# Scores of two heads: six 64-row matmuls replaced by four 128-row matmuls on stacked halves

## The chip, the cores and the metric

The kernel runs on one core of a Trainium2 chip. The metric is the device time of one execution in microseconds; the median of three runs before the change is 1390.06 us (1389.64 to 1392.08). The names of the engines in the rows: PE is TensorE, DVE is VectorE, ACT is ScalarE, POOL is GpSimd, and SP is the engine that issues the transfers.

## What is computed

A decoder trunk of two layers on a sequence of 1024 rows of width 1024, float32. Layer A is differential attention with 8 heads of two 64-wide components, layer B is stick-breaking attention with 16 heads of width 64; the kernel takes those in 8 pairs, so in either layer one unit of work ("a head" below) holds two 64-wide score products. Cut from the reference:

```python
# layer A, per block of 128 query rows: two softmaxes, one difference
def probs(qb, k):
    s = jnp.einsum('bhqd,bshd->bhqs', qb, k).astype(jnp.float32) * scale
    return jax.nn.softmax(jnp.where(mask, s, -jnp.inf), axis=-1)
a = probs(qb1, k1) - lam * probs(qb2, k2)
return jnp.einsum('bhqs,bshe->bhqe', a.astype(v.dtype), v)

# layer B, per block of 128 query rows
z = jnp.einsum('bhqd,bshd->bhqs', qb, k).astype(jnp.float32) * scale
log_beta = jax.nn.log_sigmoid(z)
log_1mb = jnp.where(mask, jax.nn.log_sigmoid(-z), 0.0)
suffix = lax.cumsum(log_1mb, axis=3, reverse=True) - log_1mb
a = jnp.where(mask, jnp.exp(log_beta + suffix), 0.0)
return jnp.einsum('bhqs,bshe->bhqe', a.astype(v.dtype), v)
```

Around them stand an input norm and projections to q, k, v and a gate, and an output projection that is added to the residual. Layer B's keys and values come from a projection of the residual after layer A.

## The kernel before

Every float32 product is made of three products of a narrower 4-byte type (F32R): each operand is split into a high part (ACT copies it into F32R) and a low part (DVE subtracts the copy from the original), and high by high, high by low and low by high are added in PSUM; low by low is left out. A projection group (`group`, L567) is 24 such matmuls of 512 columns or 24 of 256 columns into one of two PSUM banks ("proj").

Work goes head by head. While one head's attention runs, the projections of the next head are merged between its steps as filling for PE. A head's attention is four units m of two blocks of query rows each; `unit_s` makes scores and the row work of DVE and ACT, `unit_t` transposes the result and multiplies it with v. `VISITS` (L612) cuts the scores of a head into ten visits: five of one block with 512 key columns, three of one block with 384, and two of two blocks (256 and 256 columns, and again 256 and 256). A visit is one filling of the PSUM tile `sc` (two banks, one for each 64-wide component).

`scores` (L619) issues a visit as six matmuls per block. The two components c lie on partitions 0 to 63 and 64 to 127 (`HI`), so each matmul uses 64 rows of the array, and the two of one term stand side by side on the two halves of it: three terms by two components. A trace row such as `sc<-kh,q 64*128 64x512 x2` is one term of both components. After the visit `evac` empties the banks: in layer A with one DVE instruction per component, in layer B with ACT copies, one for both components where the block is at most 512 columns long, else one per component.

q and k come from `split_q` and `split_k` (L657, L660): one ACT copy and one DVE subtraction each on all 128 partitions for 512 columns, twice per head for q and twice for k. The sources are PSUM banks: `tr` (transposed rows) in layer A, `proj` in layer B.

The order on every engine is set before the run by a planner (`Order.issue`, L271): it gives each operation a duration (`cost`, L240), walks through time, and lets each engine take the ready operation of the lowest number; buffers of a pool are handed out in order and block what finds none free. For PE it adds 0.42 us to each group that begins with a 64-row matmul (L200). A `rec.together()` block is one operation for it and stays in one piece. Buffers that the change touches: `o` (attention output and gate, 6), `small` (8), `zl` in layer A (score rows, 6), `q` (4 per part), `sc` (one tile of two banks).

Of the kernel before, what the change touches and what calls it, by code (L numbers as in the profile page):

```python
# [25 lines left out]
HALF = 512  # L26
EPS = 1e-6
BIG = 1.0e30
# [4 lines left out]
def f32(ap):  # L33
    return ap.bitcast(F32)
# [345 lines left out]
def build(tc, ins, out):  # L380
    nc = tc.nc
    rec = Order(tc, {"pe": nc.tensor, "act": nc.scalar, "dve": nc.vector, "pool": nc.gpsimd, "sp": nc.sync})
    act, dve, pool, pe, sp = (rec.engine(e) for e in ("act", "dve", "pool", "pe", "sp"))
# [3 lines left out]
    w_vg, w_qk, w_kv, w_b = ins["w_vg"], ins["w_qk"], ins["w_kv"], ins["w_b"]  # L387

    mk = lambda name, bufs, **kw: ctx.enter_context(tc.tile_pool(name=name, bufs=bufs, **kw))
    B = {"proj": 2, "sc": 2, "tr": 3, "av": 1, "th": 3, "g2ka": 2, "g2kb": 3, "o": 6, "w": 8, "raw": 4, "ta": 1, "g1k": 2, "hpr": 1, "small": 8, "qk": 2, "hpe": -1, "hpw": -1,  # L390
         "al": 6, "bl": 8, "tb": 3, "oa": 0, "la": 0, "lb": 8, "lt": 0, "lead": 1.0, "leada": 0.02, "leadb": 0.02, "leadxa": 0.15, "leadxb": 0.1, "holda": 0, "holdb": 0, "c2": 1, "gca": 0, "gcb": 0, "prea": 2, "preb": 1, "warm": 16, "wp": 2, "hpx": -1, "nx": 1, "nk": 6, "hpo": 0, "ob": 2, "late": 400, "ahead": 0}
    ORDERS = ((0, 1, 2, 3), (3, 0, 2, 1), (1, 3, 0, 2), (2, 0, 3, 1), (3, 2, 1, 0), (1, 2, 0, 3), (0, 2, 1, 3), (2, 3, 0, 1),
              (1, 0, 3, 2), (3, 2, 0, 1), (2, 3, 1, 0), (1, 0, 2, 3))
    cp = mk("const", 1)
# [31 lines left out]
    def fixed(pool, shape, dt, name):  # L426
        return L(Root(shape, dt, "sbuf", pool, real=pools[pool].tile(shape, dt, name=name)))
# [1 line left out]
    def kept(shape, name):  # L429
        return L(Root(shape, F32, "dram", "dr", real=dr.tile(shape, F32, name=name)))  # L430

    zt = lambda: T("zl", [P, S], B["al"], pool=layer[0])

    def zbt():

        return T("zl", [P, S + 4], B["bl"], pool=layer[0])

    def zat(n):
        return zt()

    t1k = lambda: T("t1k", [P, 256], B["ta"], pool=layer[0])
    g1k = lambda: T("g1k", [P, 256], B["g1k"], pool=layer[0])
    u4k = lambda: T("u4k", [P, S], B["tb"], pool=layer[0])
    g2k = lambda: T("g2k", [P, HALF], B["g2k" + "ab"[layer[1]]], pool=layer[0])
    small = lambda n: T("small", [P, 16], B["small"])[:, :n]

    def C(name, shape, dt=F32):
        return fixed("cp", shape, dt, name)
# [8 lines left out]
    mask_a = fixed("la", [P, HALF], mybir.dt.bfloat16, "mask_a")  # L457
    pool.memset(mask_a, 0.0)
    pool.affine_select(mask_a[:, 384:], mask_a[:, 384:], [[-1, P]], ALU.is_ge, BIG, base=0, channel_multiplier=1)


    warm = PS("tr", B["tr"])
# [155 lines left out]

    def scores(hd, visit, evac):  # L619

        n_t[0] += 1
        pts = T("sc", [P, 2, 512], 1, pool="ps")
        col = 0
        with rec.together():
            for i, off, w in visit:
                rs_ = slice((i % 4) * P, (i % 4) * P + P)
                q, wm = hd.q[i // 4], max(w, 256)
                for a, b in ((0, 0), (0, 1), (1, 0)):
                    for c in range(2):
                        pe.matmul(pts[:, c, col:col + wm], q[a][HI[c], rs_], hd.k[b][HI[c], off:off + wm], start=(a + b == 0),  # L630
                                  stop=(a == 1))
                col += wm
        col = 0
        for i, off, w in visit:
            evac(i, off, w, pts[:, :, col:col + w])
            col += max(w, 256)

    def s_steps(hd, m, evac, chain):
# [7 lines left out]

        return [(sum(4 * w * 0.42 for _, _, w in visit), lambda v=visit, d=done: step(v, d)) for visit, done in VISITS[m]]

    def split_rows(h, l, pt, scale):

        act.activation(h, pt, AF.Copy, scale=1.0 if scale is None else scale)
        if scale is None:
            dve.tensor_tensor(l, pt, f32(h), ALU.subtract)
        else:
            dve.scalar_tensor_tensor(l, pt, scale, f32(h), ALU.mult, ALU.subtract)

    def split_k(k, sl, pt, scale):  # L657
        split_rows(k[0][:, sl], k[1][:, sl], pt, scale)

    def split_q(q, pt, scale):  # L660
        split_rows(q[0], q[1], pt, scale)

    def transposed(ae, ao, t, last):

# [86 lines left out]
            hd.k = (T("kh", [P, S], 2, F32R), T("kl", [P, S], 2, F32R))  # L751

    def alloc_q(hd, hf):
        hd.q[hf] = [T(f"q{i}", [P, HALF], 4, F32R) for i in range(2)]
        return hd.q[hf]

    def gate_steps(hd, xT, r):
# [16 lines left out]
    class OutProj:  # L774
# [43 lines left out]
        def load_rest(self):  # L818
            w = {}
            for kc in range(self.nk, KC):  # L820
                w[kc] = [T(t, [P, HALF], 4, F32R) for t in ("q0", "q1")]
                k = slice((kc - 6) * 256, (kc - 5) * 256)
                if layer[1]:
                    for i in range(2):
                        sp.dma_start(f32(w[kc][i]).rearrange("p (c n) -> p c n", c=2),
                                          self.w_out[0:2, i, :, kc * 256:(kc + 1) * 256].rearrange("c p n -> p c n"))
                    continue
                split_w([t.unsqueeze(1) for t in w[kc]], self.w_out[0:2, 3, :, k].rearrange("c p n -> p c n"))
            return w
# [193 lines left out]
    def unit_s_a(h, m):  # L1023
        hd = heads_a[h]

        def evac(qb, off, w, pts):
            n = (qb + 1) * P
            if qb not in hd.rows:
                hd.rows[qb] = [zat(n + P), zat(n + P)], [small(2), small(2)]
            p, mn = hd.rows[qb]  # L1030
            k = 0 if off == 0 else 1
            mask = mask_a[:, HALF - w:] if off + w == n else mask_a[:, 0:1].to_broadcast([P, w])
            for c in range(2):
                dve.tensor_tensor_reduce(p[c][:, off:off + w], pts[:, c, :], mask, 1.0, BIG, ALU.add, ALU.min,
                                         mn[c][:, k:k + 1])

        def chain(qb):
            n = (qb + 1) * P
            p, mn = hd.rows[qb]
            s = small(2)  # L1040
            for c in range(2):
                b = mn[c][:, 0:1]
                if n > 512:
                    dve.tensor_tensor(b, b, mn[c][:, 1:2], ALU.min)
                act.activation(p[c][:, :n], p[c][:, :n], AF.Exp, bias=b, scale=-1.0, accum_out=s[:, c:c + 1])
            r = small(2)
            dve.reciprocal(r, s)
            dve.tensor_tensor(r[:, 1:2], r[:, 1:2], nlam, ALU.mult)
            dve.tensor_scalar(p[0][:, :n], p[0][:, :n], r[:, 0:1], None, ALU.mult)
            dve.scalar_tensor_tensor(p[1][:, :n], p[1][:, :n], r[:, 1:2], p[0][:, :n], ALU.mult, ALU.add)  # L1050
            hd.at[qb] = p[1]

        return s_steps(hd, m, evac, chain)
# [68 lines left out]
        split_x(1, i)  # L1122
    squares(1)

    cst = zt()
    sp.dma_start(cst[:, :256], ins["rope"])
    sp.dma_start(cst[:, 256:544], ins["rows"].to_broadcast([P, 288]))
    rope = cst[:, :256].rearrange("p (r i d) -> p r i d", r=8, i=2)
# [104 lines left out]
    def unit_s_b(p, m):  # L1233
        hd = heads_b[p]

        def evac(qb, off, w, pts):
            n = (qb + 1) * P
            heads = ((0, 1),) if n <= HALF else ((0,), (1,))
            w2 = len(heads[0]) * n
            if qb not in hd.rows:  # L1240
                hd.rows[qb] = [zbt() for _ in heads]
                for t in hd.rows[qb]:
                    pool.memset(t[:, w2:w2 + 1], 0.0)
            for t, cs in zip(hd.rows[qb], heads):
                t3 = t[:, :w2].rearrange("p (c n) -> p c n", c=len(cs))
                with hp():
                    act.activation(t3[:, :, off:off + w], pts[:, cs[0]:cs[-1] + 1, :], AF.Copy)
                if off + w == n:
                    pool.affine_select(t3[:, :, n - P:], t3[:, :, n - P:], [[0, len(cs)], [-1, P]], ALU.is_ge, -BIG,
                                       base=-1, channel_multiplier=1)  # L1250

        def chain(qb):
            n = (qb + 1) * P
            z = hd.rows[qb]
            w2 = n * 2 // len(z)
            for t in z:
# [100 lines left out]
```

## Time and profile before

| | |
|---|---|
| median of three runs | 1390.06 us |
| the profiled execution | 1398.29 us |
| its span, first to last instruction | 1396.4 us |
| mean granted TensorE clock over it | 0.99 of full |
| busy: PE / DVE / ACT / POOL | 97% / 78% / 64% / 26% |
| chain of work that ended last, share on PE | 69% |

The profiled execution is 8.2 us longer than the median run. PE's busy share counts the pipelined tail of a matmul as busy, so how fast PE works is read from the distance between the starts of neighbouring matmuls, not from their durations. Nearly all rows carry the line L377, since one statement issues everything; tiles tell the groups apart.

### The profile page before, as it was taken

Reading aid. Unit: us, or ns where it says so; the run is one execution under the profiler, and the core shown is the slowest. Engines: PE = TensorE matmul, PEld = TensorE weight load, DVE = VectorE, ACT = ScalarE, POOL = GpSimd, SP = SyncE. Lnnn points to the kernel's source line nnn. Section 1 sums busy time; section 2 is a strip of 40 time slices with the busy share of each in tenths; the row PEclk is TensorE's granted clock in tenths of the full one; section 3 lists DMA queues with packets and bytes.
Section 4 is the critical chain, followed back from the end, with each engine's and each line's share of the span. In section 5 each row is a group of like instructions: output and inputs, shape, how many; then the busy total and the mean of one; then the engine's idle time right before and its main releaser. Section 6 shows DMA issues by size and latency. Waiting matters only on the chain.

```text
span 1396.4 us, 23006 instructions
## 1 busy us (share of the span) xinstructions
PE 1360.2 (97%) x8160; PEld 1126.5 (81%) x8160; DVE 1091.8 (78%) x2015; ACT 889.2 (64%) x1734; POOL 364.0 (26%) x589
## 2 busy tenths in 40 slices
PE   8999999999999999999899999999999999999988
PEld 7998979797979788768787878778787878788767
DVE  7689798888888987766744789797979696989771
ACT  7476657666767575533325687787778786877540
POOL 4412232322223223103201132332324142323100
PEclk8999999999999999999999999999999999999999
DMA  5255546554646465651523112121212121156624
GB/s 190 69 174 174 181 139 195 166 175 149 203 147 188 151 214 191 204 199 61 174 68 121 61 69 84 61 91 61 91 61 91 61 90 51 62 190 216 231 80 139
DMA packets 99395, 185.83 MB, mean 133 GB/s; under 512 B 8912, under 2 KB 43472, under 8 KB 98256
## 3 DMA queue, kind: packets, MB, share of 16 engines
q1 hardware_dynamic: 99280, 184.35, 40.3%
q8 instruction: 65, 1.06, 0.3%
q14 instruction: 50, 0.41, 0.1%
HBM read 119.31 MB, written 65.01 MB: 132 GB/s over the span
## 4 chain that ended last, share of the span: by engine, by line
PE 69%; DVE 15%; ACT 5%; DMA 4%; issue 4%; POOL 2%; SPq 0%; DVEq 0%; POOLq 0%; ACTq 0%
PE proj L377 46%; PE av L377 8%; PE tr L377 8%; PE sc L377 7%; DVE u4k L377 6%; DVE zl L377 3%; ACT zl L377 2%; DMA w_b<-raw 1%; DVE tl L377 1%; DVE o L377 1%; DVE small L377 1%; POOL qk L377 1%; ACT u4k L377 1%; DMA raw<-in_b_w_out_dram 1%; DMA raw<-in_w_b_dram 1%
## 5 line engine op out<-in xcount | busy, mean ns | idle before, releaser
L377 PE MATMUL proj<-ah,w 128*128 128x512 f32 x2016 | 701.3, 405 | 7.5 <-DVE w L377 2.2
L377 PEld LDWEIGHTS proj<-ah,w 128*128 128x128 f32 x2016 | 381.3, 189 | 99.4 <-issue 15.9
L377 PE MATMUL proj<-al,w 128*128 128x512 f32 x1008 | 396.5, 393 | 0.2 <-DVE al L377 0.2
L377 PEld LDWEIGHTS proj<-al,w 128*128 128x128 f32 x1008 | 191.6, 190 | 29.8 <-DVE al L377 0.5
L377 PE MATMUL proj<-w,ah 128*128 128x256 f32 x1024 | 198.4, 292 | 1.2 <-ACT ah L377 0.7
L377 DVE TENSOR_TENSOR_SCAN u4k<-zl,u4k 128x768 f32<-128x768 f32 (+4 forms) x96 | 181.5, 1891 | 3.1
L377 DVE TENSOR_TENSOR tl<-tr,th 128x512 fp32r<-128x512 f32 (+1 forms) x240 | 144.9, 629 | 42.7 <-ACT th L377 39.4
L377 PEld LDWEIGHTS proj<-w,ah 128*128 128x128 f32 x1024 | 162.0, 194 | 6.8 <-issue 4.1
L377 ACT ACTIVATE u4k<-u4k 128x768 f32<-128x768 f32 (+4 forms) x192 | 158.3, 841 | 7.3 <-DVE u4k L377 4.9
L377 ACT ACTIVATE th<-tr 128x512 fp32r<-128x512 f32 (+1 forms) x240 | 124.9, 549 | 50.6 <-PE tr L377 44.8
L377 PE MATMUL av<-th,v 128*128 128x256 f32 x640 | 152.4, 293 | 4.7 <-ACT th L377 2.8
L377 PE MATMUL proj<-w,al 128*128 128x256 f32 x512 | 147.1, 287 | 1.8 <-DVE al L377 1.5
L377 PE MATMUL sc<-kh,q 64*128 64x512 f32 (+2 forms) x768 | 140.2, 382 | 1.0 <-DVE small L377 1.0
L377 PE MATMUL av<-tl,v 128*128 128x256 f32 x480 | 130.7, 292 | 7.8 <-DVE tl L377 7.5
L377 PEld LDWEIGHTS av<-th,v 128*128 128x128 f32 x640 | 111.4, 191 | 24.2 <-issue 7.1
L377 PE MATMUL tr<-ident,zl 128*128 128x128 f32 x864 | 128.8, 274 | 1.3 <-DVE zl L377 0.8
L377 PEld LDWEIGHTS tr<-ident,zl 128*128 128x128 f32 x864 | 101.3, 141 | 14.7 <-issue 4.4
L377 DVE SCALAR_TENSOR_TENSOR u4k<-zl,u4k 128x768 f32<-128x768 f32 (+4 forms) x96 | 94.2, 981 | 23.6 <-ACT u4k L377 22.6
L377 POOL TENSOR_SCALAR_AFFINE_SELECT zl<-zl 128x128 f32<-128x128 f32 (+1 forms) x96 | 71.9, 766 | 154.6 <-ACT zl L377 136.3
L377 POOL TENSOR_TENSOR o<-o,o 128x512 f32<-128x512 f32 (+1 forms) x56 | 87.5, 1562 | 93.0 <-DVE o L377 93.0
L377 PEld LDWEIGHTS sc<-kh,q 64*128 64x128 f32 x768 | 69.8, 184 | 49.5 <-issue 25.1
L377 DVE CUSTOM_DVE_ANT_0 zl<-sc,mask_a 128x384 f32<-128x384 f32 (+3 forms) x192 | 99.4, 550 | 12.2 <-PE sc L377 12.0
(136 smaller groups left out, 2005.5 us busy)
## 6 DMA issues: line engine op xcount, KB each, us to landing
w_kv<-raw SPq DMA_DIRECT2D x64, 256.0 KB, 2.7
w_b<-raw SPq DMA_DIRECT2D x64, 256.0 KB, 3.0
w<-w_kv SPq DMA_DIRECT2D x32, 512.0 KB, 5.3
w<-w_b SPq DMA_DIRECT2D x32, 512.0 KB, 4.9
w<-w_o SPq DMA_DIRECT2D x24, 512.0 KB, 6.0
raw<-in_w_kv_dram SPq DMA_DIRECT2D x32, 256.0 KB, 2.9
raw<-in_w_b_dram SPq DMA_DIRECT2D x32, 256.0 KB, 2.9
w_o<-raw SPq DMA_DIRECT2D x32, 256.0 KB, 3.3
```

The lines of the kernel that those rows point to most:

```text
L377: getattr(e, method)(*[real(x) for x in a], **{k: real(v) for k, v in kw.items()})
```

## The change

For each component c the two halves of the 128 partitions are now both used for one product. k of component c is one tile of 128 rows: its high part on c's own half, its low part on the other half. q of component c is two tiles: `padded[..][c]` has the high part on c's half and zeros on the other (written once at the start), and `q{c}` has the low part on c's half and a second copy of the high part on the other half. The tile `q{c}` against k gives low by high plus high by low in one matmul, the padded tile against k gives high by high: two matmuls of 128 rows per block and component, four for both in place of six of 64 rows.

The copy of q's high part on the other half is made by a transfer issued on SP from the first one's partitions (64 partitions of 512 columns, 128 KB). Splitting q or k takes two ACT copies and two DVE subtractions on 64 partitions in place of one and one on 128. `sc` is two tiles of one bank, each emptied on its own; in layer B every evacuation is one ACT copy per component. Buffer counts change: `o` 6 to 4, layer A's score rows 6 to 2 and 3 (one pool per component), q 4 to 3 per part (with three padded pairs beside them), `small` 8 to three pools of 4. The planner's order follows from all this.

```diff
@@ buffers @@
-    zt = lambda: T("zl", [P, S], B["al"], pool=layer[0])
-    def zat(n):
-        return zt()
+    def zat(c):
+        return T(("z0", "z1")[c], [P, S], B[("z0", "z1")[c]], pool=layer[0])
...
+    n_q = [0]
+    padded = [[fixed("cp", [P, HALF], F32R, f"qz{i}{c}") for c in range(2)] for i in range(B["qz"])]
+    for pad in padded:
+        for c, rows in ((0, slice(64, 128)), (1, slice(0, 64))):
+            pool.memset(f32(pad[c][rows]), 0.0)
@@ scores @@
-        n_t[0] += 1
-        pts = T("sc", [P, 2, 512], 1, pool="ps")
-        col = 0
-        with rec.together():
+        pts = [T("sc", [P, 512], B["sc"], pool="ps") for _ in range(2)]
+        for c in range(2):
+            col = 0
             for i, off, w in visit:
                 rs_ = slice((i % 4) * P, (i % 4) * P + P)
-                q, wm = hd.q[i // 4], max(w, 256)
-                for a, b in ((0, 0), (0, 1), (1, 0)):
-                    for c in range(2):
-                        pe.matmul(pts[:, c, col:col + wm], q[a][HI[c], rs_], hd.k[b][HI[c], off:off + wm], start=(a + b == 0),
-                                  stop=(a == 1))
+                q, wm = hd.q[i // 4][c], max(w, 256)
+                with rec.together():
+                    for b in range(2):
+                        pe.matmul(pts[c][:, col:col + wm], q[b][:, rs_], hd.k[c][:, off:off + wm], start=(b == 0), stop=(b == 1))
                 col += wm
@@ splits @@
-    def split_rows(h, l, pt, scale):
-        act.activation(h, pt, AF.Copy, scale=1.0 if scale is None else scale)
+    def minus(l, pt, scale, h):
         if scale is None:
             dve.tensor_tensor(l, pt, f32(h), ALU.subtract)
         else:
             dve.scalar_tensor_tensor(l, pt, scale, f32(h), ALU.mult, ALU.subtract)
     def split_k(k, sl, pt, scale):
-        split_rows(k[0][:, sl], k[1][:, sl], pt, scale)
+        for c in range(2):
+            a, b = HI[c], HI[1 - c]
+            act.activation(k[c][a, sl], pt[a], AF.Copy, scale=1.0 if scale is None else of(scale, a))
+            minus(k[c][b, sl], pt[a], of(scale, a), k[c][a, sl])
     def split_q(q, pt, scale):
-        split_rows(q[0], q[1], pt, scale)
+        for c in range(2):
+            a, b = HI[c], HI[1 - c]
+            act.activation(q[c][1][a], pt[a], AF.Copy, scale=1.0 if scale is None else of(scale, a))
+            sp.dma_start(f32(q[c][0][b]), f32(q[c][1][a]))
+            minus(q[c][0][a], pt[a], of(scale, a), q[c][1][a])
...
     def alloc_q(hd, hf):
-        hd.q[hf] = [T(f"q{i}", [P, HALF], 4, F32R) for i in range(2)]
+        hd.q[hf] = [(T(f"q{c}", [P, HALF], B["q"], F32R), padded[n_q[0] % len(padded)][c]) for c in range(2)]
+        n_q[0] += 1
@@ layer B, evac @@
-                    act.activation(t3[:, :, off:off + w], pts[:, cs[0]:cs[-1] + 1, :], AF.Copy)
+                    for j, c in enumerate(cs):
+                        act.activation(t3[:, j, off:off + w], pts[c], AF.Copy)
```

How the order moves is shown at three places. First PE, the first visit of the sixth head pair of layer B, before (`tr` transposes the row work of the pair before, `av` multiplies with v, `proj` is the filling):

```order
L377 MATMUL tr_12898<-ident,zl_12363 128x128
L377 MATMUL sc_12904<-kh_12183,q_2429_12586 128x384 x2
L377 MATMUL sc_12904<-kl_12205,q_2429_12586 128x384 x2
L377 MATMUL sc_12904<-kh_12183,q_2430_12597 128x384 x2
L377 MATMUL av_12924<-th_12781,v_11593 128x256
L377 MATMUL proj_12926<-ah_8411,w_12446 128x512
```

The same place on PE now (`kh` and `kl` are the stacked k of the first and the second component, `q` the tile with low and copied high part, `qz` the padded one):

```order
L377 MATMUL tr_12918<-ident,zl_12308 128x128
L377 MATMUL sc_12922<-kh_12189,q_2429_12610 128x384
L377 MATMUL sc_12922<-kh_12189,qz_82 128x384
L377 MATMUL sc_12932<-kl_12194,q_2430_12616 128x384
L377 MATMUL sc_12932<-kl_12194,qz_83 128x384
L377 MATMUL proj_12942<-ah_8366,w_12451 128x512
```

Three paired terms have become four single matmuls; what stands before and behind is of the same kind.

Second DVE, in layer B around the second split of k of that head pair, before (`u4k` is the row work of stick-breaking, `tl` the low part of transposed rows):

```order
L377 SCALAR_TENSOR_TENSOR u4k_12197<-zl_12019,u4k_12197 128x768 x2
L377 SCALAR_TENSOR_TENSOR u4k_12210<-zl_12021,u4k_12210 128x1024 x2
L377 TENSOR_TENSOR kl_12205<-proj_12177,kh_12183 128x512
L377 TENSOR_TENSOR tl_12236<-tr_12214,th_12224 128x384
L377 TENSOR_TENSOR tl_12321<-tr_12240,th_12268 128x512
```

And now:

```order
L377 SCALAR_TENSOR_TENSOR u4k_12217<-zl_12032,u4k_12217 128x768 x2
L377 SCALAR_TENSOR_TENSOR u4k_12227<-zl_12035,u4k_12227 128x1024 x2
L377 TENSOR_TENSOR kh_12189<-proj_12185,kh_12189 64x512
L377 TENSOR_TENSOR kl_12194<-proj_12185,kl_12194 64x512
L377 TENSOR_TENSOR o_11962<-av_12257,o_11962 64x256
L377 TENSOR_TENSOR tl_12348<-tr_12252,th_12285 128x512
```

One subtraction has become two, at the same place in the queue, ahead of the same `tl` work.

Third PE, among the last head pair's scores of the program, before:

```order
L377 MATMUL sc_15039<-kh_13816,q_2761_14524 128x512 x2
L377 MATMUL proj_15022<-ah_14307,q_2841_14507 128x512
L377 MATMUL proj_15022<-al_14322,q_2841_14507 128x512
L377 MATMUL proj_15022<-ah_14307,q_2842_14528 128x512
L377 MATMUL proj_15028<-ah_14307,q_2841_14507 128x512
L377 MATMUL proj_15028<-al_14322,q_2841_14507 128x512
L377 MATMUL proj_15028<-ah_14307,q_2842_14528 128x512
L377 MATMUL sc_15060<-kh_13816,q_2760_14503 128x512 x2
```

And now, where `av_15059` belongs to the same head pair (here `q_2760` and `q_2761` are q tiles; in the rows above `q_2841` and `q_2842` are pieces of the output weights that use the same pool):

```order
L377 MATMUL sc_15054<-kh_13821,q_2760_14501 128x512
L377 MATMUL sc_15054<-kh_13821,qz_80 128x512
L377 MATMUL av_15059<-th_14975,v_14088 128x256
L377 MATMUL av_15059<-tl_14984,v_14088 128x256
L377 MATMUL av_15059<-th_14975,v_14088 128x256
L377 MATMUL av_15059<-tl_14984,v_14088 128x256
L377 MATMUL sc_15066<-kl_13828,q_2761_14519 128x512
L377 MATMUL sc_15066<-kl_13828,qz_81 128x512
L377 MATMUL sc_15071<-kh_13821,q_2760_14501 128x512
L377 MATMUL sc_15071<-kh_13821,qz_80 128x512
```

Here the projection pieces that stood between the visits stand behind all of them now; seven visits follow each other with only `av` work between.

## Rows read from the trace of the kernel before

**Rows 1.** Page, part 1: busy time, share and instructions of each engine.
```profile
PE 1360.2 (97%) x8160; PEld 1126.5 (81%) x8160; DVE 1091.8 (78%) x2015; ACT 889.2 (64%) x1734; POOL 364.0 (26%) x589
```

**Rows 2.** Waits of PE: total us, times, longest; the largest of 15.
```profile
PE av L377 <- DVE tl L377: 7.5, 14, 2.1
```

**Rows 3.** Windows: stretch, its us, busy us by engine; a head in either layer.
```profile
408.00:480.00 72.00, 70.98 (x489) 61.15 (x488) 60.88 (x154) 46.15 (x106) 19.99 (x24) 1.00 0.56 174
...
982.00:1056.00 74.00, 73.03 (x425) 58.72 (x424) 62.58 (x77) 57.91 (x100) 23.80 (x47) 1.00 0.22 72
```

**Rows 4.** Timeline of PE: start us, us, what; a visit of 512 columns.
```profile
462.20 0.39 PE L377 MATMUL proj<-al,w 128*128 128x512 f32 x1
462.43 0.39 PE L377 MATMUL proj<-ah,w 128*128 128x512 f32 x1
462.75 0.50 PE L377 MATMUL sc<-kh,q 64*128 64x512 f32 x2
463.08 0.40 PE L377 MATMUL sc<-kl,q 64*128 64x512 f32 x2
463.31 0.40 PE L377 MATMUL sc<-kh,q 64*128 64x512 f32 x2
463.64 0.50 PE L377 MATMUL proj<-ah,w 128*128 128x512 f32 x1
463.98 0.40 PE L377 MATMUL proj<-al,w 128*128 128x512 f32 x1
```

**Rows 5.** Timeline of PE, a visit of 384 columns with its neighbours.
```profile
960.69 0.39 PE L377 MATMUL proj<-ah,w 128*128 128x512 f32 x1
960.92 0.49 PE L377 MATMUL tr<-ident,zl 128*128 128x128 f32 x3
961.34 0.44 PE L377 MATMUL sc<-kh,q 64*128 64x384 f32 x2
...
962.06 0.38 PE L377 MATMUL av<-th,v 128*128 128x256 f32 x1
962.29 0.40 PE L377 MATMUL proj<-ah,w 128*128 128x512 f32 x1
```

**Rows 6.** Timeline of PE, a visit of two blocks of 256 columns.
```profile
928.84 0.40 PE L377 MATMUL proj<-ah,w 128*128 128x512 f32 x1
...
930.07 0.50 PE L377 MATMUL proj<-ah,w 128*128 128x512 f32 x1
930.41 0.40 PE L377 MATMUL proj<-al,w 128*128 128x512 f32 x1
```

**Rows 7.** Groups by shape, DVE: count, busy us, mean ns, idle before.
```profile
L377 DVE TENSOR_TENSOR o<-av,o 64x256 f32<-64x256 f32 x64 | 26.6, 415 | 8.9 <-ACT o L377 7.7
L377 DVE TENSOR_TENSOR v<-tr,v 128x256 fp32r<-128x256 f32 x32 | 13.0, 408 | 7.7 <-ACT v L377 7.5
...
L377 DVE SCALAR_TENSOR_TENSOR q<-tr,cols,q 128x512 fp32r<-128x512 f32 x16 | 12.0, 747 | 6.8 <-ACT q L377 6.8
...
L377 DVE SCALAR_TENSOR_TENSOR q<-proj,q 128x512 fp32r<-128x512 f32 x16 | 11.0, 685 | 2.6 <-ACT q L377 2.6
```

**Rows 8.** Groups by shape, ACT.
```profile
L377 ACT ACTIVATE zl<-sc 128x512 f32<-128x512 f32 x72 | 39.2, 592 | 3.1 <-PE sc L377 2.9
...
L377 ACT ACTIVATE q<-tr,cols 128x512 fp32r<-128x512 f32 x16 | 11.0, 686 | 33.7 <-PE tr L377 33.7
...
L377 ACT ACTIVATE zl<-sc 128x1024 f32<-128x1024 f32 x8 | 8.1, 1015 | 0.4 <-PE sc L377 0.4
```

**Rows 9.** Windows of 3.7 us in a head of layer B, two of twenty.
```profile
982.00:985.70 3.70, 3.45 (x21) 2.53 (x20) 3.67 (x8) 3.30 (x6) 1.59 (x5) 1.00 0.01 4
...
1022.70:1026.40 3.70, 3.70 (x25) 3.31 (x24) 0.56 (x1) 1.40 (x5) 2.07 (x12) 1.00 0.00 0
```

**Rows 10.** DMA issues: out<-in, count, KB each, median us to landing.
```profile
og_b<-o SPq DMA_DIRECT2D x28, 256.0 KB, 2.1
...
q<-w_o SPq DMA_DIRECT2D x4, 256.0 KB, 6.3
```

More of the change, by code (lines that the diff above doesn't have):

```diff
@@ L389, in build @@
     mk = lambda name, bufs, **kw: ctx.enter_context(tc.tile_pool(name=name, bufs=bufs, **kw))
-    B = {"proj": 2, "sc": 2, "tr": 3, "av": 1, "th": 3, "g2ka": 2, "g2kb": 3, "o": 6, "w": 8, "raw": 4, "ta": 1, "g1k": 2, "hpr": 1, "small": 8, "qk": 2, "hpe": -1, "hpw": -1,
-         "al": 6, "bl": 8, "tb": 3, "oa": 0, "la": 0, "lb": 8, "lt": 0, "lead": 1.0, "leada": 0.02, "leadb": 0.02, "leadxa": 0.15, "leadxb": 0.1, "holda": 0, "holdb": 0, "c2": 1, "gca": 0, "gcb": 0, "prea": 2, "preb": 1, "warm": 16, "wp": 2, "hpx": -1, "nx": 1, "nk": 6, "hpo": 0, "ob": 2, "late": 400, "ahead": 0}
+    B = {"proj": 2, "sc": 2, "tr": 3, "av": 1, "th": 3, "g2ka": 2, "g2kb": 3, "o": 4, "w": 8, "raw": 4, "ta": 1, "g1k": 2, "hpr": 1, "small": 4, "qk": 2, "hpe": -1, "hpw": -1,
+         "al": 6, "bl": 8, "tb": 3, "oa": 0, "la": 0, "lb": 8, "lt": 0, "lead": 1.0, "leada": 0.02, "leadb": 0.02, "leadxa": 0.15, "leadxb": 0.1, "holda": 0, "holdb": 0, "c2": 1, "gca": 0, "gcb": 0, "prea": 2, "preb": 1, "warm": 16, "wp": 2, "hpx": -1, "nx": 1, "nk": 6, "hpo": 0, "ob": 2, "late": 400, "ahead": 0, "q": 3, "qz": 3, "z0": 2, "z1": 3}
     ORDERS = ((0, 1, 2, 3), (3, 0, 2, 1), (1, 3, 0, 2), (2, 0, 3, 1), (3, 2, 1, 0), (1, 2, 0, 3), (0, 2, 1, 3), (2, 3, 0, 1),
@@ L444, in build @@
     g2k = lambda: T("g2k", [P, HALF], B["g2k" + "ab"[layer[1]]], pool=layer[0])
-    small = lambda n: T("small", [P, 16], B["small"])[:, :n]
+    small = lambda n, tag=None: T(tag or "small", [P, 2 if tag else 16], B["small"])[:, :n]
     def C(name, shape, dt=F32):
@@ L634, in scores @@
         for i, off, w in visit:
-            evac(i, off, w, pts[:, :, col:col + w])
+            evac(i, off, w, [t[:, col:col + w] for t in pts])
             col += max(w, 256)
@@ L655, in split_rows, with of @@
             dve.scalar_tensor_tensor(l, pt, scale, f32(h), ALU.mult, ALU.subtract)
+    def of(scale, rows):
+        return scale[rows] if isinstance(scale, L) else scale
     def split_k(k, sl, pt, scale):
-        split_rows(k[0][:, sl], k[1][:, sl], pt, scale)
+        for c in range(2):
+            a, b = HI[c], HI[1 - c]
+            act.activation(k[c][a, sl], pt[a], AF.Copy, scale=1.0 if scale is None else of(scale, a))
+            minus(k[c][b, sl], pt[a], of(scale, a), k[c][a, sl])
     def split_q(q, pt, scale):
-        split_rows(q[0], q[1], pt, scale)
+        for c in range(2):
[3 more added lines that the diff above has]
+            minus(q[c][0][a], pt[a], of(scale, a), q[c][1][a])
     def transposed(ae, ao, t, last):
@@ L820, in load_rest @@
             for kc in range(self.nk, KC):
-                w[kc] = [T(t, [P, HALF], 4, F32R) for t in ("q0", "q1")]
+                w[kc] = [T(t, [P, HALF], B["q"], F32R) for t in ("q0", "q1")]
                 k = slice((kc - 6) * 256, (kc - 5) * 256)
@@ L1028, in evac @@
             if qb not in hd.rows:
-                hd.rows[qb] = [zat(n + P), zat(n + P)], [small(2), small(2)]
+                hd.rows[qb] = [zat(0), zat(1)], [small(2, "min"), small(2, "min")]
             p, mn = hd.rows[qb]
@@ L1033, in evac @@
             for c in range(2):
-                dve.tensor_tensor_reduce(p[c][:, off:off + w], pts[:, c, :], mask, 1.0, BIG, ALU.add, ALU.min,
+                dve.tensor_tensor_reduce(p[c][:, off:off + w], pts[c], mask, 1.0, BIG, ALU.add, ALU.min,
                                          mn[c][:, k:k + 1])
@@ L1039, in chain @@
             p, mn = hd.rows[qb]
-            s = small(2)
+            s = small(2, "sum")
             for c in range(2):
@@ L1045, in chain @@
                 act.activation(p[c][:, :n], p[c][:, :n], AF.Exp, bias=b, scale=-1.0, accum_out=s[:, c:c + 1])
-            r = small(2)
+            r = small(2, "sum")
             dve.reciprocal(r, s)
@@ L1123, in build @@
     squares(1)
-    cst = zt()
+    cst = zat(0)
     sp.dma_start(cst[:, :256], ins["rope"])
```

## The prediction

> **What bounds the kernel now.** The busy table is read first [rows 1]: PE is at 97% with 1360.2 us, so in the whole run it idles for 36.2 us, while DVE has 1091.8 us and ACT 889.2. The list of PE's waits is second [rows 2]: its longest entry is 7.5 us in 14 pieces, waits of `av` for the low part that DVE writes. The windows over one head say the same of either layer [rows 3]: PE busy 70.98 of 72 us in A and 73.03 of 74 us in B, DVE 60.88 and 62.58, ACT 46.15 and 57.91. So PE is the bound in the 16 heads, and what PE's own stream gets shorter by, the run gets shorter by, as long as DVE, with 11.1 and 11.4 us free per head, keeps up. Since a busy PE is counted with its pipelined tails, the price of a visit has to come from starts of matmuls in the timeline.
>
> **The visits on PE.** In a run of projections one 512-column matmul follows the other after 0.23 us, as from 462.20 to 462.43 [rows 4]. Over a 512 visit the distance between the starts of the two projections on both sides of it, with the one directly behind, is 463.98 - 462.43 = 1.55 us; two projections take 0.46 of it, so the visit costs 1.09 us. Three paired terms at 0.23 would be 0.69. The other 0.40 lies at the borders and is seen piece by piece in the same rows: 0.32 instead of 0.23 before the first term, 0.33 after the first, 0.33 after the last, 0.34 after the first projection behind, while the middle pair has 0.23. Changes among 128-row work show nothing like that: a projection is followed by transposes after 0.23, from 960.69 to 960.92 [rows 5].
>
> - 512 columns: now four matmuls of 128 rows at the projections' 0.23, 0.92 us. Gain 1.09 - 0.92 = 0.17.
> - 384 columns: 962.29 - 961.34 = 0.95 with one `av` in it, which at half of a 512 matmul is 0.115; with the 0.09 ahead of the first term as in the 512 visit the visit is 0.925 [rows 5]. Now four times three quarters of 0.23, 0.69. Gain 0.235.
> - two blocks of 256: 930.41 - 928.84 - 0.46 = 1.11 [rows 6]. Now eight times 0.115, 0.92. Gain 0.19.
>
> `VISITS` has 5, 3 and 2 of them per head, 80, 48 and 32 in the 16 heads of both layers: 13.6 + 11.3 + 6.1 = 31 us less on PE. No row shows a score with 128 rows; that it runs like a projection of the same columns and type is the assumption, and the rounding of the starts is worth about 3 us either way.
>
> On these rows the Trainium skill has two rules. The middle pair's 0.23 for two 64-row matmuls is the pace that the Trainium skill, TensorEngine Tiling (Array Packing), section Theoretical Speedup, promises for a contraction of at most 64 (up to twofold); by that rule alone the change goes from three passes to four and loses. The Trainium skill, same page, section Key Properties, says that a change of the tiling mode drains the array; the 0.40 us at the borders agrees with it, and by both rules together the sum is the one above.
>
> **What the change adds.** DVE: a split on 64 partitions does not get shorter, since 64x256 takes 415 ns and 128x256 takes 408 [rows 7]. Of the 64 splits (16 heads, q and k, two halves each) every one gets a second subtraction: in A 32 times 0.747, in B 32 times 0.685 (the k ones taken like the q ones), 23.9 + 21.9 = 45.8 us, 3.0 per head in A and 2.7 in B. ACT: 64 more copies at no more than 0.686, 44 us, and in B four visits' worth of one-piece evacuations per head become two, 2 x 0.592 - 1.015 = 0.17 for the widest and the same taken for the others, 32 x 0.17 = 5 us [rows 8]. ACT keeps over 10 us free per head in B and over 20 in A; cost nothing, and if its cover were gone it would act through the same waits as DVE's.
>
> DVE's cover is its free time. A head gets 31/16 = 1.9 us shorter, so in A 60.9 + 3.0 of 70.1 us are busy, in B 62.6 + 2.7 of 72.1: free 6.2 and 6.8 us in place of 11.1 and 11.4. A queue in front of a server whose free time shrinks by a factor of 1.7 to 1.8 makes its customers wait longer by about that factor. On the wait for DVE's low part [rows 2] that is +6 us; on all of PE's idle time, 36.2 us, it is +29; below, 0, since the planner places PE's filling by the same extra DVE work (in the order, `tl` work stands behind both subtractions and PE has other matmuls between). I take +8, near the row that names DVE.
>
> The rest I take as nothing, from -4 to +6 together:
> - The 64 transfers of 128 KB. The nearest in the trace are 256 KB in 2.1 to 6.3 us [rows 10]. Behind q's projection PE still has the gate's two groups, 48 matmuls of 0.23, 11 us, even in the first head of a layer, and about a quarter to half of a head later on. So the first score waits only if the issue is held up: SP works in order, and a copy queued behind a load that waits for a buffer, or a load behind a copy that waits for ACT (0.6 to 0.7 us), pushes the next.
> - `sc` in two tiles lets DVE or ACT begin after two matmuls, and frees one bank while the other is being emptied: a small gain.
> - Fewer buffers for `o`, q and score rows: a second row of the next unit in A waits until the unit before is transposed. PE has filling in 15 of 16 heads. In the last head of B the order shows seven visits in a row without projections; ACT empties one of 512 columns in 2 x 0.592 = 1.18 us where PE makes it in 0.92, so PE waits some 2 us there, and has the projections for the later stretch where it had been waiting before.
> - The zeros are written once at the start.
>
> Sum: -31 + 8 = -23 us. Against the profiled execution, 1398.3, that is 1375; the median run is 8.2 us shorter, and the same difference taken from it gives 1390.1 - 23 = 1367 us.
>
> **Rivals.**
> 1. The gain is eaten in the stretches where DVE is full. Of the twenty pieces of a B head, 13 have DVE busy for 3.5 of 3.7 us or more, as the first one of those shown has, and others next to none (0.56 at 1022.70) [rows 9]. If what lands in full stretches, 13/20 of 45.8 = 30 us, all comes out as PE waiting, nothing is left: 1389 us. For it: the full stretches are there. Against: PE today runs through them with about 1 us of waiting per head, since it has the next head's projections.
> 2. DVE becomes the bound: its whole 45.8 us against PE's 31, +15 us, 1405 us. It decides once two thirds of the added DVE time turns into PE waiting, that is once DVE's queue never runs empty in a head. Against: 6 to 7 us per head stay free on average.
> 3. The borders stay. If the 0.40 us belongs to something that four full matmuls also pay (new weights of another kind, the bank's hand-over), four passes replace three: 0.23 x 80 + 0.17 x 48 + 0.23 x 32 = 34 us more, 1424 us. (It is what the Trainium skill, TensorEngine Tiling (Array Packing), section Theoretical Speedup, would make of the change if it stood alone.) Against: the same weights and banks change hands between projections and transposes without it [rows 5].
>
> **How the numbers follow.** What this measurement can tell from no change is about 0.2%, 2.8 us. The forecast, PE's gain with some more waiting, gets 0.80; its own range is 1355 to 1380 (-34 to -10). Rival 1 gets 0.12, half of it a little faster and half within 0.2%; rival 2 0.05, rival 3 0.03. Faster: 0.80 + 0.04 of rival 1, 0.84; within: 0.08; slower: 0.08. The range runs from -36, a gain with no added wait and a small one from the score banks, to the no-change end of rival 1: 1354 to 1390.
>
> **What would show it.** In the timeline a 512 visit should take 0.92 us from its first start to the next work's and the projections beside it 0.23; 0.33 at its edges would speak for rival 3. The head period should fall from 74.0 to about 72.5 us in B and from 72 to 70.5 in A. PE's waits for `tl` should stay under some 15 us in sum, DVE's busy time rise to about 1137 us; if DVE is at 3.6 of 3.7 us in nearly all pieces of a head, rival 1 or 2 holds. Waits of `sc` for the copied half, more than a few us, would make the transfer's cover wrong.

## The result

The changed kernel takes 1377.47 us (median of four runs, 1375.14 to 1379.39) beside 1391.07 us for the kernel before in the same comparison: a ratio of 0.9900 (95% interval 0.9878 to 0.9923), 13.6 us less. The forecast was 1367 us. A second set of five runs gave 1379.36 us, ratio 0.9898 (0.9881 to 0.9914).

The profiled executions differ by more, 1398.29 and 1375.14 us. The former is slower than all four timed runs of its kernel (1389.64 to 1393.25), the latter the fastest of its own, and the granted clock explains most of it: 0.990 over a span of 1396.4 us is 14.0 us short of full speed, 0.996 over 1373.4 us is 5.5. So of the 23.0 us between the spans some 8 are clock, and the change itself is worth 13 to 15 in either way of counting.

### The profile after

Engines of the changed kernel, and the largest waits of PE; they answer to [rows 1, 2]:

```profile
PE 1334.1 (97%) x7776; PEld 1161.6 (85%) x7776; DVE 1134.5 (83%) x2079; ACT 937.6 (68%) x1830; POOL 349.6 (25%) x595
```
```profile
PE av L377 <- DVE tl L377: 10.7, 12, 1.6
PE proj L377 <- DVE al L377: 3.5, 6, 0.8
PE sc L377 <- ACT zl L377: 3.4, 7, 0.6
PE av L377 <- ACT th L377: 2.4, 6, 1.2
PE sc L377 <- DVE min L377: 2.2, 4, 1.1
```

PE's share is the same as before, with 26.1 us less busy time. DVE has 42.7 us more, ACT 48.4. No copied half of q is in the list of what PE waited for.

A visit of 512 columns between projections, the start of the next work after a 384 visit, and a visit of two blocks, as [rows 4 to 6] show them of before (start us, us, what):

```profile
738.56 0.39 PE L377 MATMUL proj<-ah,w 128*128 128x512 f32 x1
738.79 0.40 PE L377 MATMUL sc<-kh,q 128*128 128x512 f32 x1
739.02 0.39 PE L377 MATMUL sc<-kh,qz 128*128 128x512 f32 x1
739.25 0.40 PE L377 MATMUL sc<-kl,q 128*128 128x512 f32 x1
739.49 0.40 PE L377 MATMUL sc<-kl,qz 128*128 128x512 f32 x1
739.72 0.39 PE L377 MATMUL proj<-ah,w 128*128 128x512 f32 x1
739.95 0.39 PE L377 MATMUL proj<-al,w 128*128 128x512 f32 x1
```
```profile
735.32 0.34 PE L377 MATMUL sc<-kh,q 128*128 128x384 f32 x1
...
736.03 0.39 PE L377 MATMUL proj<-ah,w 128*128 128x512 f32 x1
```
```profile
604.24 0.28 PE L377 MATMUL sc<-kh,q 128*128 128x256 f32 x1
...
605.19 0.40 PE L377 MATMUL proj<-ah,q 128*128 128x512 f32 x1
605.42 0.40 PE L377 MATMUL proj<-al,q 128*128 128x512 f32 x1
```

From start to start the visits take 0.93, 0.71 and 0.95 us, and every neighbour keeps its 0.23: the 0.32 to 0.34 at the borders are gone. It holds over all visits: the median of what a distance at their edges has above the pace of its columns is 0.006 us or less, and was 0.09 to 0.11 at each of four places before (a pair taken as one). The Trainium skill, TensorEngine Tiling (Array Packing), section Key Properties, says that a change of the tiling mode drains the array. The rows agree with it: without a change of mode, no border.

So the visits gave what was forecast. Where the rest went is seen when the span is cut at the first score of head 0, of head 7 (the last of layer A), of head 8 (the first of layer B) and of head 15. Windows of before: the seven periods of layer A, then the seven of layer B (columns as in [rows 3]):

```profile
67.70:567.60 499.90, 493.22 (x3376) 424.15 (x3375) 425.43 (x1064) 322.75 (x729) 131.37 (x162) 1.00 0.55 175
...
746.40:1258.40 512.00, 506.84 (x2919) 406.50 (x2919) 424.87 (x517) 398.49 (x687) 153.16 (x310) 1.00 0.24 81
```

The same of the changed kernel:

```profile
65.80:567.30 501.50, 489.90 (x3220) 441.30 (x3220) 459.52 (x1100) 347.54 (x760) 129.13 (x166) 1.00 0.59 183
...
735.30:1234.60 499.30, 493.54 (x2749) 425.93 (x2748) 435.57 (x541) 415.95 (x738) 141.11 (x309) 1.00 0.28 89
```

The clock is full in all four. Layer B went from 512.0 to 499.3 us, 1.8 us per head, as forecast. Layer A went from 499.9 to 501.5: **nothing of the 13.6 us forecast for its seven heads was kept.** DVE is the first difference that the rows show: in A it is now busy for 459.5 of 501.5 us, 92% (85% before), in B 87% (83%). Its busy time grew by 34.1 us in A and by 10.7 in B, though the forecast's prices add 20.9 and 19.2 there: rows that the change leaves alone became longer in A and shorter in B (the passes `u4k<-zl` of B fell from 67.5 to 58.2 us in the whole run).

How A lost it is counted from the starts of matmuls. Above the plain pace (0.2275, 0.172, 0.119 and 0.109 us for 512, 384, 256 and 128 columns, half of that for 64-row matmuls) the distances at score matmuls, with that of the first matmul behind them, had 29.9 us in A before and 29.6 in B; 28.4 of these are the borders of 70 visits (five of 0.41, three of 0.40 and two of 0.40 per head). After it is 13.0 us in A and 1.3 in B. So B has no new wait at its scores, and A some 12 us. Ten places of A with over 0.25 us make 8.3 of them, and in six of the ten it is an `av` that stands directly behind a score pair and waits for `tl`. The longest, in rows of PE, DVE and POOL:

```profile
274.06 0.68 DVE L377 CUSTOM_DVE_ANT_0 z<-sc,mask_a 128x512 f32<-128x512 f32 x1
...
274.67 2.01 DVE L377 TENSOR_TENSOR w<-raw,w 128x512 fp32r<-128x512 f32 x2
...
276.01 1.79 POOL L377 TENSOR_TENSOR o<-g2k,o 128x512 f32<-128x512 f32 x1 [0.48 <-POOL o L377]
...
276.40 0.28 PE L377 MATMUL sc<-kh,q 128*128 128x256 f32 x1
...
276.52 0.28 PE L377 MATMUL sc<-kh,qz 128*128 128x256 f32 x1
276.61 1.22 DVE L377 TENSOR_TENSOR min<-min 128x1 f32<-128x1 f32 x1
277.74 0.55 DVE L377 TENSOR_TENSOR tl<-tr,th 128x384 fp32r<-128x384 f32 x1
...
278.44 0.36 PE L377 MATMUL av<-tl,v 128*128 128x256 f32 x1 [1.64 <-DVE tl L377]
```

DVE works without a gap from 274.06; `tl` comes after two splits of weights and a `min` that took 1.22 us (its 64 average 243 ns), and PE stands still for 1.8 us behind the second score matmul. In A, DVE empties the score banks besides (`z<-sc`); in B, ACT does that.

That `min` works on one column, and its length goes with GpSimd: it ends at 277.82, 0.02 us after GpSimd's row `o<-g2k,o` that ran when it began. Of the 64 `min` rows nine take more than 0.3 us, and all nine end 0.01 to 0.02 us after a GpSimd row of the same kind (tensor by tensor) that ran when they began; of the other 55 none takes more than 0.17 us. Before, one of 64 was so long, and it lies behind the seven periods of A. Five of the nine stand directly ahead of the `tl` of five of the six `av` waits. These five waits are 5.5 of A's some 12 us, and 3.5 of them are the time by which the five `min` rows are longer than the usual 0.155 us (an estimate from these rows, the rest taken as it is). So part of A's loss comes from where GpSimd's rows fall, not from the sum of DVE's work. No run moved GpSimd's rows.

The added DVE and ACT work has the sizes of [rows 7, 8]:

```profile
L377 DVE SCALAR_TENSOR_TENSOR q<-tr,cols,qz 64x512 fp32r<-64x512 f32 x32 | 24.0, 750 | 5.1 <-ACT qz L377 4.3
...
L377 DVE SCALAR_TENSOR_TENSOR q<-proj,qz 64x512 fp32r<-64x512 f32 x32 | 22.0, 686 | 6.4 <-ACT qz L377 5.0 <-PE av L377 0.9
```

And the copies, beside [rows 10]:

```profile
q<-qz SPq DMA_DIRECT2D x64, 128.0 KB, 2.3
```

### The profile page after: what moved, and what is told of

The parts are those of the page before. It is cut to its first block, busy times and chain, and to the rows that moved or that the text cites. A ratio compares the mean times of both kernels' runs of the same rounds, so it can differ in the third digit from the quotient of the medians.

```text
span 1373.4 us, 22565 instructions
## 1 busy us (share of the span) xinstructions
PE 1334.1 (97%) x7776; PEld 1161.6 (85%) x7776; DVE 1134.5 (83%) x2079; ACT 937.6 (68%) x1830; POOL 349.6 (25%) x595
## 4 chain that ended last, share of the span: by engine, by line
PE 61%; DVE 21%; ACT 10%; DMA 4%; issue 3%; POOL 1%; SPq 0%; DVEq 0%; ACTq 0%; POOLq 0%
PE proj L377 42%; PE av L377 7%; PE tr L377 7%; DVE z L377 5%; PE sc L377 5%; DVE u4k L377 4%; ACT u4k L377 2%; DVE tl L377 2%; ACT zl L377 1%; DVE w L377 1%; ACT qz L377 1%; DVE raw L377 1%; ACT z L377 1%; DVE v L377 1%; DVE o L377 1%
## 5 line engine op out<-in xcount | busy, mean ns | idle before, releaser
L377 PEld LDWEIGHTS proj<-al,w 128*128 128x128 f32 x1008 | 190.2, 189 | 29.9 <-DVE al L377 0.5
L377 DVE TENSOR_TENSOR_SCAN u4k<-zl,u4k 128x768 f32<-128x768 f32 (+4 forms) x96 | 176.3, 1837 | 3.0
L377 PE MATMUL av<-th,v 128*128 128x256 f32 x640 | 147.0, 284 | 3.3 <-ACT th L377 2.4
L377 PE MATMUL av<-tl,v 128*128 128x256 f32 x480 | 128.7, 289 | 11.1 <-DVE tl L377 10.7
L377 ACT ACTIVATE z<-z,min 128x256 f32<-128x256 f32 (+7 forms) x128 | 98.6, 771 | 59.8 <-DVE min L377 59.5
L377 DVE CUSTOM_DVE_ANT_0 z<-sc,mask_a 128x384 f32<-128x384 f32 (+3 forms) x192 | 102.8, 550 | 14.3 <-PE tr L377 7.5
L377 PEld LDWEIGHTS av<-tl,v 128*128 128x128 f32 x480 | 90.8, 189 | 21.6 <-DVE tl L377 11.3
L377 PEld LDWEIGHTS proj<-w,al 128*128 128x128 f32 x512 | 98.1, 192 | 4.8 <-DVE al L377 4.8
L377 ACT ACTIVATE zl<-u4k 128x768 f32<-128x768 f32 (+4 forms) x96 | 81.5, 849 | 30.0 <-DVE u4k L377 29.8
L377 ACT ACTIVATE zl<-sc 128x384 f32<-128x384 f32 (+3 forms) x192 | 82.8, 494 | 20.9 <-PE sc L377 17.1
## 6 DMA issues: line engine op xcount, KB each, us to landing
w<-w_kv SPq DMA_DIRECT2D x32, 512.0 KB, 5.3
w<-w_b SPq DMA_DIRECT2D x32, 512.0 KB, 5.0
w<-w_o SPq DMA_DIRECT2D x24, 512.0 KB, 4.9
```

The lines of the kernel that those rows point to most:

```text
L377: getattr(e, method)(*[real(x) for x in a], **{k: real(v) for k, v in kw.items()})
```

## The experiments

Three theories on what was missing against the forecast. Theory 1: the borders are gone, and the loss is PE waiting for a fuller DVE. Theory 2: the smaller buffer counts cost it. Theory 3: the new score banks or the transfers do. All times in one table; "A" and "B" are the seven periods of each layer in the profiled execution, "rest" what remains of its span. The clock is full in A and B, except that plan_dve_cost loses 6.8 us to it in A (mean granted clock 0.99), and order_38, order_42, dve_relief, act_relief, banks_joined and copy_on_act 1.7 us in B. Kernels are compared by the ratio or with after_again, which ran beside the first of them.

| run | median us | ratio to before (95%) | A | B | rest |
|---|---|---|---|---|---|
| before | 1391.07 | 1 | 499.9 | 512.0 | 384.5 |
| after | 1377.47 | 0.9900 (0.9878 to 0.9923) | 501.5 | 499.3 | 372.6 |
| after_again | 1379.36 | 0.9898 (0.9881 to 0.9914) | 502.9 | 499.2 | 375.5 |
| buffers_alone | 1396.72 | 1.0023 (1.0013 to 1.0033) | 503.3 | 511.5 | 379.4 |
| banks_joined | 1389.15 | 0.9971 (0.9958 to 0.9984) | 501.6 | 510.6 | 374.8 |
| dve_relief | 1373.25 | 0.9858 (0.9839 to 0.9876) | 494.0 | 500.9 | 374.8 |
| pe_less | 1339.09 | 0.9611 (0.9598 to 0.9624) | 480.6 | 473.4 | 383.2 |
| act_relief | 1383.50 | 0.9933 (0.9921 to 0.9945) | 500.7 | 509.2 | 373.3 |
| plan_dve_cost | 1403.50 | 1.0078 (1.0065 to 1.0092) | 504.2 | 500.2 | 399.9 |
| gate_on_act | 1372.69 | 0.9849 (0.9835 to 0.9863) | 497.2 | 501.5 | 374.2 |
| order_38 | 1391.14 | 0.9997 (0.9984 to 1.0010) | 506.8 | 508.2 | 375.3 |
| order_42 | 1376.59 | 0.9886 (0.9873 to 0.9898) | 498.9 | 503.6 | 372.1 |
| before_42 | 1387.38 | 0.9961 (0.9948 to 0.9974) | 497.6 | 509.3 | 378.0 |
| copy_on_act | 1405.31 | 1.0089 (1.0077 to 1.0101) | 514.5 | 514.7 | 374.6 |

The three order runs came last and change how the others are read, so they stand first.

### Other orders of the same instructions

In each, the planner's margin is changed and nothing else; `order_38` and `order_42` are the kernel after, `before_42` the kernel before.

```diff
-MARGIN = 0.4
+MARGIN = 0.38        # order_38; 0.42 in order_42 and before_42
```

> The kernel after with the same instructions, tiles and buffer counts; only the planner's margin of time after the end of an operation's inputs is 0.38 in place of 0.4 us, which gives another order on every engine. The theory under test is that a measured difference is the change's own and not the luck of one order: within 4 us of after (1374 to 1383 us). The rival, that the order chosen for after is a lucky or unlucky one: off by 8 us or more, and then the experiments that moved the time by 4 to 7 us (fewer buffers, the added subtractions, the added copies, the gate's copies) can't be read as single causes.

> As the run with margin 0.38, here 0.42 us: a second order of the same instructions. Within 4 us of after if the size of the change belongs to the change; off by 8 us or more if it belongs to the order.

> The kernel before with the margin 0.42 us: another order of its instructions. If orders are worth little, within 4 us of before (ratio 0.997 to 1.003). The rival, that the order of before is one that fits its planner's costs unusually well: slower by 8 us or more; part of the gain that after lacks against the forecast would then be the fit of the order of before, which after does not have.

The run with 0.42 lies within 4 us of after, as the theory said; the one with 0.38 is 12 to 14 us slower, as the rival said. So the rival holds: the same instructions in another order take 1376.6 to 1391.1 us, a spread of 14.5 us, as large as the change. The kernel before, for which only the same or a slower time had been expected, has an order that is 4.8 us better than its own. So the 13.6 us belong to this pair of orders; the mean of three orders after (1381.7 us) is 8 us under the mean of two before (1389.8 with 1392.2 for before in that comparison). Where the spread lies is in the heads, PE's work being the same. Layers A and B of `order_38`:

```profile
66.60:573.40 506.80, 493.82 (x3221) 441.16 (x3221) 462.02 (x1100) 350.11 (x761) 130.30 (x166) 1.00 0.58 180
...
743.90:1252.10 508.20, 496.86 (x2749) 426.80 (x2748) 442.43 (x542) 417.82 (x738) 148.65 (x309) 1.00 0.27 87
```

And its waits in layer B, where the kernel after has 5.7 us of `tl`:

```profile
PE av L377 <- DVE tl L377: 10.1, 7, 2.5
```

What the layers say stands in every order tried: B is faster after (499.3, 503.6, 508.2) than before (509.3, 512.0), though by 1.1 us only at the closest; A is not (498.9, 501.5, 506.8 beside 497.6, 499.9). In both layers the three orders after stand in the sequence of DVE's busy time: 456.4, 459.5 and 462.0 us in A (margin 0.42, 0.4 and 0.38), 435.6, 438.7 and 442.4 in B (0.4, 0.42 and 0.38). The instructions are the same, so what differs is how long they took and how far they overlap. The orders differ by 9 us in B and 8 in A, and an experiment that moves a layer by less than that can't be read by itself.

### The same kernel again

No edit.

> The changed kernel again, for the interval and as the base of its variants. Between the first and the last matmul its trace has 34 us more of plain matmul pace than before, 47 us less at the edges of visits and elsewhere, and 8 us less lost to low clock. Theory 1 (border costs gone, about -30 us; more PE waiting since DVE and ACT are fuller, about +14 us): 1376 us, 15 us less than before. Theory 2 (the missing part of the gain is paid for fewer buffers) and theory 3 (paid for the transfer and the two score banks) expect the same here.

The layers come again within 1.4 us and the median within 1.9. The spread of orders is no spread of runs.

### Fewer buffers alone

```diff
-"o": 6, ... "small": 8,
+"o": 4, ... "small": 4, "z0": 2, "z1": 3}    # three pools of 4 for small; q 4 to 3 per part
```

> The kernel before with only the changed buffer counts (o 4, q 3, score rows 2 and 3, the small ones in three pools of 4). Theory 1: no change, within 3 us of before. Theory 2: most of the missing 14 us, 1400 to 1405 us. Theory 3: no change.

The kernel before with the new counts is 4 us slower than before, 3.4 of it in layer A, whose score rows are what became fewer. That is more than the 3 us of theory 1 and short of the 1400 us of theory 2. Theory 2 can hold for a few us there; a change of order alone has moved A by more.

### One score tile of two banks again

```diff
-pts = [T("sc", [P, 512], B["sc"], pool="ps") for _ in range(2)]
+pt2 = T("sc", [P, 2, 512], 1, pool="ps")
+pts = [pt2[:, c, :] for c in range(2)]
...
-                    for j, c in enumerate(cs):
-                        act.activation(t3[:, j, off:off + w], pts[c], AF.Copy)
+                    act.activation(t3[:, :, off:off + w], pts[:, cs[0]:cs[-1] + 1, :], AF.Copy)
```

> The changed kernel with the score PSUM as one tile of two banks again, and one ACT copy for both components in layer B's short blocks: 32 ACT copies fewer (5 us of ACT), but a visit is emptied only when both components are there. Theory 1: within 4 us of the changed kernel, rather slower. Theory 3: 5 to 10 us faster.

10 us slower than after_again, all of it in B (510.6 beside 499.3), where above the plain pace the distances at scores grow from 1.3 to some 15 us. Theory 3 had 5 to 10 us faster, so it falls for the banks; theory 1 had at most 4 us slower. That the separate banks bring 10 us is likely from the place, not certain beside the orders' 9 us: this order also has DVE busy for 448.8 us in B beside 435.6, with 752 ns for the mean pass `u4k<-zl` beside 641.

### Half of the subtractions left out

```diff
 def split_k / split_q, for each component c
-            minus(...)
+            if c == 0: minus(...)
+            else: pool.memset(low part, 0.0)
```

> The changed kernel without the subtractions of the second component of q and k (64 of 128; POOL writes zeros there, so the second component's low parts are left out of the scores): DVE has 46 us less, the rest stands. Theory 1: most of the extra waiting goes, 8 to 14 us faster than the changed kernel, 1363 to 1369 us, DVE busy about 1089 us. Theories 2 and 3: within 3 us of the changed kernel.

A falls by 7.5 us to 494.0, B stays (+1.6). The windows of A and B:

```profile
66.90:560.90 494.00, 488.61 (x3220) 441.79 (x3219) 435.25 (x1068) 348.90 (x760) 140.26 (x191) 1.00 0.59 185
730.20:1231.10 500.90, 495.31 (x2749) 427.40 (x2748) 416.96 (x515) 414.95 (x740) 153.83 (x334) 1.00 0.28 88
```

With 24 us less on DVE in A, a third comes back; with 19 less in B, nothing. The whole run is 6.1 us faster than after_again, less than the 8 to 14 that theory 1 announced. It is theory 1's pattern in A, with a size that an order could also make.

### The gate's copies on ACT in place of DVE

```diff
-"gca": 0, "gcb": 0
+"gca": 1, "gcb": 1     # L784: act.copy instead of dve.tensor_copy, 28 pieces
```

> The changed kernel with the 28 copies of the gated output (0.53 us each) on ACT in place of DVE: DVE 15 us less, ACT 17 us more. Theory 1 with DVE as the dearer engine: 1 to 3 us faster than the changed kernel. If ACT's load costs as much: no change.

The same pattern from another side: A 497.2 (-4.3), B 501.5 (+2.2). At 1372.69 us it is the fastest kernel of this study that leaves nothing out, 1.5% under before. The 6.7 us against after_again are more than the 1 to 3 announced; against the best order of after (1376.59) it is 3.9 us ahead, less than an order is worth.

### Half of the scores' matmuls left out

```diff
-for b in range(2):
-    pe.matmul(pts[c][:, col:col + wm], q[b][:, rs_], hd.k[c][:, off:off + wm], start=(b == 0), stop=(b == 1))
+pe.matmul(pts[c][:, col:col + wm], q[0][:, rs_], hd.k[c][:, off:off + wm], start=True, stop=True)
```

> The changed kernel with one of the two score matmuls per block and component (high by high is left out): 384 matmuls fewer, 68 us less of PE's stream, DVE and ACT as they are. If PE is still what bounds the heads: 1310 to 1320 us. If DVE and ACT now bound them (DVE 1135 us plus the stretches at the layers' ends where it waits): 1350 us or more.

By the plain pace 29.8 us leave PE in each layer. B gives back 25.9 of them, A 20.9; the whole run 40 of 68. With 1339 us it lies between the two forecasts, 1310 to 1320 and 1350 or more; outside the heads it is 10.6 us longer than after, of which some 9 are clock (mean granted 0.989 beside 0.996). Since most of the 29.8 us come back, PE still sets the time in both layers, far above the orders' spread; the 5 us by which A gives back less are not.

### Half of the copies on ACT left out

As in the run with half of the subtractions, but with `act.activation` for component 0 only and zeros for the other.

> The changed kernel without ACT's copies of the second component of q and k (64 of 128; POOL writes zeros there, so that component's high parts are left out of the splits): ACT has 41 us less, DVE and PE as they are. Theory 1 (waits come from the fuller engines, ACT as well as DVE): 3 to 6 us faster than the changed kernel. Rival (ACT at 68% hides it all): within 2 us of it.

4 us slower than after_again, with 41 us less on ACT: A unchanged, B +9.9. Neither forecast had it slower. No sign that the added ACT work costs anything; the loss in B is of the size of an order.

### The planner's DVE durations raised to the measured ones

```diff
-return 0.06 + 0.0021 * n, 0.15
+return 0.1 + 0.0023 * n, 0.15      # and likewise the other DVE forms
```

> The changed kernel with the planner's durations for DVE raised to what the trace shows (a 1024-column sign pass 0.94 in place of 0.68, the scan 2.45 in place of 2.21, a 512-column subtraction 0.68 in place of 0.60): same instructions, another order. If the waits of PE come from DVE running behind the planned order: 4 to 10 us faster than the changed kernel. If they come from DVE's sum alone: within 3 us of it.

The idea that a planner with truer durations would find the lost time fell: 24 us slower than after_again. Nothing of it is in the heads (A 504.2, 6.8 of which are clock; B 500.2); "rest" grew by 27. Of these, 21 lie between the layers and 6 behind the last head's first score, where the granted clock is 0.96 and 0.93, and 1.00 and 0.98 in after.

### The second copy by ACT in place of the transfer

```diff
-sp.dma_start(f32(q[c][0][b]), f32(q[c][1][a]))
+act.activation(q[c][0][b], pt[a], AF.Copy, scale=1.0 if scale is None else of(scale, a))
```

> The kernel after with the second copy of q's high half made by a third ACT copy from the PSUM bank (64 more instructions of 64x512, some 42 us on ACT) in place of the 64 transfers of SP. Theory 1, the transfers lie in the cover of PE's filling and cost nothing: 0 to 5 us slower than after, ACT busy about 980 us. The rival, the transfers hold up loads behind them on SP's queue or delay the first scores: 3 to 8 us faster than after.

26 us slower than after_again, 13.0 in A and 15.4 in B, more than the 0 to 5 of theory 1 and on the other side of the rival. In A, PE now waits for the high part that ACT copies out of the transposes:

```profile
PE av L377 <- ACT th L377: 8.5, 13, 1.4
```

In after that wait was 2.4 us there. So this way of doing without the transfers doesn't help, and the rival's 3 to 8 us did not come. It doesn't show that the transfers are free, since the ACT copies in their place cost something too; for that stands only the list of waits, in which no score waits for a copied half. How much of the 26 is the order stays open.

## Why the prediction came out as it did

**The bound**: right. PE kept 97%, and a kernel with fewer matmuls on it got faster in both layers.

**The visits on PE**: right. Forecast 0.92, 0.69 and 0.92 us, measured 0.93, 0.71 and 0.95, and no border. With the visits of [rows 4 to 6] that is 80 x 0.16 + 48 x 0.215 + 32 x 0.16 = 28 us less in place of 31. Rival 3, borders that stay, is out.

**The added work**: right in the sum, DVE +42.7 us for 45.8, ACT +48.4 for 49. For DVE the sum hides two misses that cancel: 34.1 us more in A's seven periods where the prices give 20.9, 10.7 in B's where they give 19.2.

**The wait for DVE**: here the working failed, in size and in place. It took one factor for both layers and +8 us for the run. The head period fell to 72.5 us in B, just as forecast (74.2 to 72.5 by first scores), but in A the seven periods sum to 501.5 us, 71.6 each, where 70.5 had been announced. Layer A's new waits, some 12 us at the scores and 2 elsewhere, are all but the whole gain of its heads; B has 1. What the working missed, as far as rows show it: PE's order in A puts `av` directly behind a short visit, `tl` stands behind whatever DVE has to do first, and some of that is held until a GpSimd row ends (5.5 of the 12 us lie at such places). That DVE in A also empties the score banks may add to it; no run separates that. In its size, rival 1 (the gain eaten where DVE is full) described A, the forecast described B. The rival had been read off a head of B.

The announced sign, waits for `tl` under 15 us, did not warn of it: 10.7 us stand in the list. Most of the loss shows only in starts, since a PE that is held up counts as partly busy: PE's busy time in A fell by 3.3 us, where its shorter visits say 13.

**The rest, taken as nothing**: transfers, no cost seen. SP did stand waiting for the ACT copy that a transfer reads, 125.9 us in 28 pieces and up to 18.2 us at once where 0.6 to 0.7 had been named, but no wait of PE's for a copied half came of it. Two score tiles: one bank tile again was 10 us slower, all in B, so the gain may be larger than "small". Fewer buffers: about 4 us, in A. Outside the heads the span lost 11.9 us, of which some 8 are clock.

**From the profiled execution to the median**: like with like, 28 us less on PE and about 13 to 15 more waiting give the 13.6 measured. The forecast was 10 us too low, as much as the mis-sized term (+8 for +13 to +15) and the visits (31 for 28) make.

**Luck**: the 1377 us lie in the forecast's range with this order. With margin 0.38 the same instructions take 1391 us, and the kernel before takes 1392.

What was not foreseen at all: the order that the planner happens to find is worth as much as the change. What stays open is how much of A's loss belongs to DVE's load, how much to GpSimd's rows and how much to these particular orders. Three orders and two reliefs of DVE point to DVE; no run holds the order fixed while it takes DVE's load away.

## What to carry to other kernels

Price a saving on the bound engine stage by stage, and check the load that it adds stage by stage too: the same 1.9 us per head were kept in B and lost in A, and a sum over the run (+42.7 us on DVE) hid 34 us in one layer and 11 in the other. When a scheduler sets the order, run two or three orders of both kernels before a change of 1% is called one. Here, paired 64-row matmuls among 128-row ones paid 0.40 us a visit at their borders; such a price is read start to start across the border, not from the length of the rows.

## What had not been expected of the hardware

One DVE instruction of unchanged shapes, the integer step of stick-breaking (`u4k<-zl`, 96 of them), took 730 ns on average before and 641 after, and 641 to 752 in the other runs.

```profile
L377 DVE TENSOR_SCALAR u4k<-zl 128x768 int32<-128x768 int32 (+4 forms) x96 | 58.2, 641 | 9.3 <-POOL zl L377 4.7 <-ACT zl L377 3.1 <-POOL o L377 1.4
```

A few long ones make the difference, and they go with GpSimd. Of the 96 passes after, 52 have no GpSimd row beside them, and none of these is more than 0.02 us longer than usual for its shape (51 such passes before, with the same result). Eight take over 0.3 us more (13 before), and each of them begins while GpSimd's `o<-g2k,o` or `o<-o,o` runs; five of the eight, 1024 columns wide, end 0.69 us after that row ends, which is their usual time. So these rows look like DVE waiting until GpSimd's row is done and then doing its own work, as with the `min` rows above; that GpSimd's row is the cause is read from the times alone. GpSimd's select on the same tiles is not the partner: its mean went from 766 ns before to 616 after, but in banks_joined it is 538 ns with 752 for the DVE passes.
